# Order of the half-array matmuls in a hybrid decoder layer: neighbours at other tile positions

## The chip, the core and the metric

The kernel runs on one core of one Trainium2 chip. The metric is the device time of one launch in microseconds (us). Three runs of the kernel before gave 1041.28, 1041.54 and 1042.14 us; the median is 1041.54 us.

## What is computed

One decoder layer on 1024 tokens of width 1024, in float32.

```python
h = rms_norm(x, norm_mix_g);  z = h @ w_in                 # 1024 x 1792
q, k, v, u, gate = split(z)                                # 8 query heads, 2 kv heads, 512 + 512 conv channels
a = sliding_window_gqa(rms_norm(q), rms_norm(k), v, sinks, rel_bias)
#   per block of 128 queries: scores against the block before and its own (256 keys),
#   plus bias, softmax with a sink, times v
c = silu(layer_norm(causal_depthwise_conv31(u * sigmoid(gate)) + b))
x = x + concat(rms_norm(a), rms_norm(c)) @ w_out
x = x + square(relu(rms_norm(x) @ w_up)) @ w_down          # hidden width 4096
```

## The kernel before

Everything is kept transposed: channels on the 128 partitions, tokens along the free dimension. Large products split each float32 operand into a high and a low part and use three float32r matmuls of 128x128 by 512 columns (`mm3`, `prod`); these make up nearly all of TensorE's work. Three smaller kinds of matmul are float32 and use a part of the 128x128 array. Each such float32 matmul stands in the trace as two instructions, each with its own weight load.

A matmul that reads operands from partitions 0 to 63 and writes to PSUM partitions 0 to 31 works in the part of the array at row 0, column 0. This pair of row and column is called its *tile position* here, written (row, column); it follows from the partitions that the slices in the code name.

- **Convolution** (`conv`, L423 to L450). The depthwise convolution of 128 channels is done as 64-row matmuls with 32 output partitions. There are four kinds, for r = 0, 1 (upper and lower 64 partitions) and s = 0, 1: position (64 r, 64 r + 32 s). A call makes two halves (`jh`); a half makes 16 matmuls for each of the four kinds, 64 in all, 128 instructions. They write two PSUM tiles, called x (r = 0) and o (r = 1). `conv` is called for four groups of channels, so there are 8 halves and 1024 instructions. Before them DVE transposes into `ha` (L429), and four DMAs (L430) copy parts of it to other partitions.
- **Scores** (`attn_a`, L557 to L580). A unit is one head pair j and one pair of query blocks bp; there are 16 units. A unit makes four matmuls of 64 rows and 128 columns: two blocks for kv group g = 0 at position (0, 0), two for g = 1 at (64, 0). Each group has its own PSUM tile `sc`, of which there are two. ACT and DVE then read each block (L577, L578).
- **Value products** (`attn_c`, L608 to L630). A unit makes up to eight matmuls of 128 rows and 64 columns into PSUM tile `o`: two blocks, two groups g at (0, 64 g), and two key blocks c that accumulate.

What sets the order: the string `SCHED` gives the order in which the dense work, the attention units and the norms are emitted; a list scheduler with its own model of time then places each emitted instruction in its engine's queue, by priority and by when it expects the operands. An engine takes its queue in order. So the order in the code is a wish, and the order that was built is shown below where it matters.

Of the kernel before, what the change touches and what calls it, by code (L numbers as in the profile page):

```python
# [14 lines left out]
AF = mybir.ActivationFunctionType  # L15
# [3 lines left out]
P = 128  # L19
# [48 lines left out]
class Builder:  # L68
# [354 lines left out]
    def conv(self, ct):  # L423
        nc = self.nc
        tw, ha, hg = self.tw[ct], self.ha, self.hg[ct]
        for s in range(2):
            for r in range(2):
                c0, p0 = 64 * r + 32 * s, 64 * r + 32 * (1 - s)
                nc.vector.transpose(ha[c0:c0 + 32, s].rearrange("p b j -> p (b j)"), hg[c0:c0 + 32])  # L429
                self.dma(ha[p0 + 2:p0 + 32, s, 1:NTB + 1, :], ha[c0 + 2:c0 + 32, s, 0:NTB, :])  # L430
        yt = self.tmp("yt", (P, TB, NTB))
        for jh in range(2):
            js = slice(16 * jh, 16 * jh + 16)
            ps = [self.psum("x"), self.psum("o")]
            for s in range(2):
                for j in range(16):
                    for r in range(2):
                        gp, c0 = slice(64 * r, 64 * r + 64), 64 * r + 32 * s
                        nc.tensor.matmul(ps[r][c0:c0 + 32, j * TB:(j + 1) * TB], tw[gp, s, 16 * jh + j, :],
                                         ha[gp, s, 1:NTB + 1, 16 * jh + j], start=True, stop=True)  # L440
            for r in range(2):
                gp = slice(64 * r, 64 * r + 64)
                nc.scalar.copy(yt[gp, js].rearrange("p j b -> p (j b)"), ps[r][gp])
        if ct + 1 < NCT:
            self.conv_load(ct + 1)
        src = yt.rearrange("p j b -> p b j")
        for h in range(2):
            y = self.mp.tile([P, HT], F32, tag="y", name=self.nm("y"), bufs=8)
            self.y[ct, h] = y
            nc.vector.transpose(y.rearrange("p (b t) -> p b t", t=TB), src[:, 16 * h:16 * h + 16, :])  # L450
# [106 lines left out]
    def attn_a(self, j, bp):  # L557
        nc = self.nc
        assert {j, 4} <= self.emitted
        u = dict(j=j, bp=bp, i=sum(self.n_unit))  # L560
        self.n_unit.append(1)
        u["s"] = s = self.tmp("s", (P, 4, 256))
        u["mx"] = mx = self.small("mx", 4)
        for g in range(2):
            gp = slice(64 * g, 64 * g + 64)
            psv = self.psum("sc").rearrange("p (b w) -> p b w", b=2)
            for b2 in range(2):
                b = 2 * bp + b2
                W = P if b == 0 else 2 * P
                k0 = (b + 1) * P - W  # L570
                nc.tensor.matmul(psv[:, b2, 256 - W:], self.Q[b // 4][gp, j, b % 4 * P:(b % 4 + 1) * P], self.kh[gp, k0:k0 + W],
                                 start=True, stop=True)
            for b2 in range(2):
                b = 2 * bp + b2
                W = P if b == 0 else 2 * P
                sl = s[:, 2 * b2 + g, 256 - W:]
                nc.scalar.activation(sl, psv[:, b2, 256 - W:], AF.Copy, scale=self.rq[:, j, b, g:g + 1])  # L577
                nc.vector.tensor_tensor_reduce(sl, sl, self.bias[g][:, j, 256 - W:], 1.0, NEG,  # L578
                                               ALU.add, ALU.max, mx[:, 2 * b2 + g:2 * b2 + g + 1])
        return u  # L580
# [27 lines left out]
    def attn_c(self, u):  # L608
        nc = self.nc
        s, j, bp = u["s"], u["j"], u["bp"]  # L610
        assert 5 in self.emitted
        self.n_attn[bp // 2] += 1
        po = self.psum("o")
        pT = self.tmp("pT", (P, 2, HT))
        for c in range(2):
            ps = self.psum("tr")
            i0 = 2 if bp == 0 and c == 0 else 0
            for i in range(i0, 4):
                nc.tensor.transpose(ps[:, i * P:(i + 1) * P], s[:, i, c * P:(c + 1) * P], self.ident)
            self.evac(EVAC.get(u["i"], "aaa")[c], pT[:, c, i0 * P:], ps[:, i0 * P:])  # L620
        for b2 in range(2):
            b = 2 * bp + b2
            for g in range(2):
                gp = slice(64 * g, 64 * g + 64)
                i = 2 * b2 + g
                c0 = 1 if b == 0 else 0
                for c in range(c0, 2):
                    nc.tensor.matmul(po[gp, b2 * P:(b2 + 1) * P], self.v[:, b - 1 + c, gp], pT[:, c, i * P:(i + 1) * P],
                                     start=c == c0, stop=c == 1)
        self.evac(EVAC.get(u["i"], "aaa")[2], self.Q[bp // 2][:, j, bp % 2 * 256:(bp % 2 + 1) * 256], po[:, :2 * P])  # L630
# [527 lines left out]
```

## Time and profile before

| What | Value |
|---|---|
| median of three runs | 1041.54 us |
| the profiled execution's own time | 1041.51 us |
| its span, first to last instruction | 1039.5 us |
| TensorE (PE) busy | 1009.7 us, 97% of the span |
| VectorE (DVE) busy | 676.9 us, 65% |
| ScalarE (ACT) busy | 489.9 us, 47% |
| mean granted clock of TensorE | 0.979 of full speed |

The 2.0 us between the span and the run's own time lie outside the instructions. TensorE's busy time is the union of its matmuls; matmuls overlap in it, so a busy stretch is not yet one at full pace. The granted clock has two levels, 1.00 and 0.50 in the rows (2.4 and 1.2 GHz); a value between them is a mean over a stretch with both.

### The profile page before, as it was taken

How to read it: one execution, taken by the hardware profiler on the slowest of the kernel's cores; microseconds unless marked ns; L12 is line 12 of the kernel's file. 1: busy time of each engine (PE TensorE's matmuls, PEld its weight loads, DVE VectorE, ACT ScalarE, POOL GpSimd, SP SyncE). 2: the span in 40 equal slices, each digit the busy share in tenths (PEclk: the TensorE clock that was granted, in tenths of full speed). 3: DMA queues.
4: the chain of work that ended last, by engine and by line, in shares of the span. 5: the costliest groups of instructions: out<-in, count | busy, mean ns of one | idle time of the engine just before them, and what ended most of it. 6: DMA issues, size and time to landing. Idle time of an engine off the chain costs nothing.

```text
span 1039.5 us, 14869 instructions
## 1 busy us (share of the span) xinstructions
PE 1009.7 (97%) x5552; PEld 818.4 (79%) x5552; DVE 676.9 (65%) x1148; ACT 489.9 (47%) x944; POOL 117.0 (11%) x87
## 2 busy tenths in 40 slices
PE   6999999989989989999999999999999999999998
PEld 4888887777766777877888888888888888888886
DVE  7456344346766566489778777777784677747763
ACT  5323212777756544466445445445454343443452
POOL 5000012055423530400000000000000000000000
PEclk9999999989987999999999999999999999999999
DMA  9124220000210133436465656576776542336441
GB/s 342 42 61 136 97 72 11 11 21 31 82 61 11 61 112 127 159 133 220 162 235 201 229 207 205 199 244 247 272 274 212 187 144 81 121 107 239 162 162 41
DMA packets 67752, 148.72 MB, mean 143 GB/s; under 512 B 7808, under 2 KB 8576, under 8 KB 67168
## 3 DMA queue, kind: packets, MB, share of 16 engines
q1 hardware_dynamic: 67536, 147.75, 41.5%
q8 instruction: 44, 0.72, 0.3%
q14 instruction: 28, 0.23, 0.1%
q10 hardware_dynamic: 144, 0.02, 0.0%
HBM read 106.98 MB, written 38.80 MB: 140 GB/s over the span
## 4 chain that ended last, share of the span: by engine, by line
PE 87%; DVE 6%; ACT 4%; issue 2%; DMA 1%; SPq 0%; DVEq 0%; POOL 0%; ACTq 0%; POOLq 0%
PE mm L198 7%; PE mm L200 7%; PE mm L199 6%; PE sc L841 4%; PE sc L840 4%; PE sc L842 4%; PE tr L840 3%; PE tr L841 3%; PE tr L842 3%; PE mm L840 3%; PE mm L842 3%; PE mm L841 3%; PE mm L1060 2%; PE mm L1062 2%; PE mm L1061 2%; PE sc L1062 2%
## 5 line engine op out<-in xcount | busy, mean ns | idle before, releaser
L766 ACT CAST wb<-wd 128x512 fp32r<-128x512 f32 x80 | 49.8, 622 | 111.3 <-DVE wd L1028 41.6
L767 DVE TENSOR_TENSOR wb<-wd,wb 128x512 fp32r<-128x512 f32 x80 | 55.3, 691 | 69.9 <-ACT wb L766 69.9
L200 PE MATMUL mm<-xh,wlo 128*128 128x512 f32 x192 | 77.7, 405 | 0.0
L198 PE MATMUL mm<-xh,whi 128*128 128x512 f32 x192 | 77.6, 404 | 0.0
L199 PE MATMUL mm<-xl,whi 128*128 128x512 f32 x192 | 77.2, 402 | 0.0
L767 DVE TENSOR_TENSOR wb<-hb,wb 128x512 fp32r<-128x512 f32 x112 | 76.6, 684 | 0.0
L168 DVE TENSOR_TENSOR wlo<-raw,whi 128x512 fp32r<-128x512 f32 (+1 forms) x54 | 55.0, 1019 | 33.2 <-ACT whi L167 27.9
L167 ACT CAST whi<-raw 128x512 fp32r<-128x512 f32 (+1 forms) x54 | 42.9, 795 | 68.5 <-PE mm L199 46.7
L840 PE MATMUL sc<-op,wb 128*128 128x512 f32 x192 | 74.7, 389 | 0.0
L841 PE MATMUL sc<-op,wb 128*128 128x512 f32 x192 | 74.7, 389 | 0.0
L842 PE MATMUL sc<-op,wb 128*128 128x512 f32 x192 | 74.7, 389 | 0.0
L766 ACT CAST wb<-hb 128x512 fp32r<-128x512 f32 x112 | 69.0, 616 | 0.3 <-PE sc L842 0.3
L766 ACT CAST wb<-raw 128x512 fp32r<-128x512 f32 x46 | 27.7, 621 | 65.2 <-PE tr L842 25.1
L200 PE MATMUL mm<-mix,wlo 128*128 128x512 f32 x128 | 52.1, 408 | 2.0 <-DVE wlo L168 2.0
L198 PE MATMUL mm<-mix,whi 128*128 128x512 f32 x128 | 52.9, 416 | 1.1 <-ACT x1g L766 0.7
L199 PE MATMUL mm<-mix,whi 128*128 128x512 f32 x128 | 52.1, 407 | 0.0
L1061 PE MATMUL mm<-wb,wb 128*128 128x512 f32 x128 | 49.8, 389 | 0.0
L1061 PE MATMUL sc<-wb,wb 128*128 128x512 f32 x128 | 49.8, 389 | 0.0
L840 PE MATMUL tr<-op,wb 128*128 128x512 f32 x128 | 49.8, 389 | 0.0
L841 PE MATMUL tr<-op,wb 128*128 128x512 f32 x128 | 49.8, 389 | 0.0
L1062 PE MATMUL mm<-wb,wb 128*128 128x512 f32 x128 | 49.6, 389 | 0.0
L1062 PE MATMUL sc<-wb,wb 128*128 128x512 f32 x128 | 49.6, 389 | 0.0
(270 smaller groups left out, 2595.1 us busy)
## 6 DMA issues: line engine op xcount, KB each, us to landing
hb<-hid SPq DMA_DIRECT2D x112, 256.0 KB, 2.9
wd<-w_down SPq DMA_DIRECT2D x80, 256.0 KB, 4.0
raw<-w_up SPq DMA_DIRECT2D x27, 512.0 KB, 3.6
hid<-h SPq DMA_DIRECT2D x48, 256.0 KB, 2.9
pa<-pa SPq DMA_DIRECT2D x20, 512.0 KB, 4.9
raw<-w_out SPq DMA_DIRECT2D x32, 256.0 KB, 2.6
hid<-pa SPq DMA_DIRECT2D x32, 256.0 KB, 3.0
hid<-tu SPq DMA_DIRECT2D x32, 256.0 KB, 3.7
```

Of the source, the lines that this page charges most:

```text
L167: nc.scalar.copy(hi, raw)
L168: eng.tensor_tensor(lo, raw, hi.bitcast(F32), ALU.subtract)
L198: nc.tensor.matmul(ps, w[0][:, ws], xh, start=first, stop=False)
L199: nc.tensor.matmul(ps, w[0][:, ws], xl, start=False, stop=False)
L200: nc.tensor.matmul(ps, w[1][:, ws], xh, start=False, stop=last)
L766: self.pin(self.nc.scalar.copy(hi, src))
L767: self.pin(eng.tensor_tensor(lo, src, hi.bitcast(F32), ALU.subtract))
L840: nc.tensor.matmul(ps, wh[:, c], xh, start=first and k == 0, stop=False, skip_group_check=True)
L841: nc.tensor.matmul(ps, wh[:, c], xl, start=False, stop=False, skip_group_check=True)
L842: nc.tensor.matmul(ps, wl[:, c], xh, start=False, stop=last and k == len(xs) - 1, skip_group_check=True)
L1061: nc.tensor.matmul(pss[m], wh[:, c], bl, start=False, stop=False, skip_group_check=True)
L1062: nc.tensor.matmul(pss[m], wl[:, c], bh, start=False, stop=f == NP - 1, skip_group_check=True)
```

## The change

The same matmuls with the same operands and results are issued in another order. In `conv` the loop over s moves inside the loop over j: four neighbours go to (0, 0), (64, 64), (0, 32), (64, 96), where before all 32 matmuls of s = 0 came first, alternating between (0, 0) and (64, 64), and then the 32 of s = 1. In `attn_a` both PSUM tiles are taken first and the groups alternate. In `attn_c` the loop over g moves innermost, so that neighbours go to (0, 0) and (0, 64).

```diff
@@ conv
-            for s in range(2):
-                for j in range(16):
+            for j in range(16):
+                for s in range(2):
                     for r in range(2):
                         gp, c0 = slice(64 * r, 64 * r + 64), 64 * r + 32 * s
                         nc.tensor.matmul(ps[r][c0:c0 + 32, j * TB:(j + 1) * TB], tw[gp, s, 16 * jh + j, :],
...
@@ attn_a
+        psv = [self.psum("sc").rearrange("p (b w) -> p b w", b=2) for _ in range(2)]
+        for b2 in range(2):
+            b = 2 * bp + b2
+            W = P if b == 0 else 2 * P
+            k0 = (b + 1) * P - W
+            for g in range(2):
+                gp = slice(64 * g, 64 * g + 64)
+                nc.tensor.matmul(psv[g][:, b2, 256 - W:], self.Q[b // 4][gp, j, b % 4 * P:(b % 4 + 1) * P], self.kh[gp, k0:k0 + W],
+                                 start=True, stop=True)
         for g in range(2):
-            gp = slice(64 * g, 64 * g + 64)
-            psv = self.psum("sc").rearrange("p (b w) -> p b w", b=2)
-            for b2 in range(2):
...
-                nc.tensor.matmul(psv[:, b2, 256 - W:], self.Q[b // 4][gp, j, b % 4 * P:(b % 4 + 1) * P], self.kh[gp, k0:k0 + W],
-                                 start=True, stop=True)
             for b2 in range(2):
...
@@ attn_c
-            for g in range(2):
-                gp = slice(64 * g, 64 * g + 64)
-                i = 2 * b2 + g
-                c0 = 1 if b == 0 else 0
-                for c in range(c0, 2):
+            c0 = 1 if b == 0 else 0
+            for c in range(c0, 2):
+                for g in range(2):
+                    gp = slice(64 * g, 64 * g + 64)
+                    i = 2 * b2 + g
                     nc.tensor.matmul(po[gp, b2 * P:(b2 + 1) * P], self.v[:, b - 1 + c, gp], pT[:, c, i * P:(i + 1) * P],
                                      start=c == c0, stop=c == 1)
```

The scheduler's own placing moves too. TensorE, the first half of the first convolution, before (x and o are the convolution's PSUM tiles, mm a dense one; L439 is the convolution):

```order
L198 MATMUL mm_794<-xh_253,whi_569 128x512
L439 MATMUL x_355<-ha,tw_121 32x32 x3
L439 MATMUL o_356<-ha,tw_121 32x32 x3
L439 MATMUL x_355<-ha,tw_121 32x32
L439 MATMUL o_356<-ha,tw_121 32x32
```

The same place now:

```order
L198 MATMUL mm_794<-xh_253,whi_569 128x512
L439 MATMUL x_355<-ha,tw_121 32x32
L199 MATMUL mm_794<-xl_254,whi_569 128x512
L200 MATMUL mm_794<-xh_253,wlo_570 128x512
L198 MATMUL mm_794<-xh_271,whi_569 128x512
L439 MATMUL o_356<-ha,tw_121 32x32
L199 MATMUL mm_794<-xl_272,whi_569 128x512
L200 MATMUL mm_794<-xh_271,wlo_570 128x512
L198 MATMUL mm_820<-xh_133,whi_569 128x512
L199 MATMUL mm_820<-xl_134,whi_569 128x512
L200 MATMUL mm_820<-xh_133,wlo_570 128x512
L439 MATMUL x_355<-ha,tw_121 32x32 x4
```

One matmul of x and one of o now stand alone between dense ones, and the other 62 follow together. Counted over the program, the convolution's matmuls stood in 10 uninterrupted runs (64, 64, 64, 64, 64, 64, 47, 17, 5 and 59 long) and stand in 18 now (1, 1, 62, 64, 64, 2, 62, 64, 64, 2, 21, 41, 1, 11, 19, 2, 1 and 30).

TensorE, the first unit's scores (sc, L571), before, where g = 0 (sc_1753) and g = 1 (sc_1760) stand in one run after the convolution:

```order
L505 MATMUL tr_1583<-bones,sq_1524 128x2 x4
L571 MATMUL sc_1753<-kh,Q_497 128x128
L571 MATMUL sc_1753<-kh,Q_497 128x256
L571 MATMUL sc_1760<-kh,Q_497 128x128
L571 MATMUL sc_1760<-kh,Q_497 128x256
L198 MATMUL mm_1555<-xh_253,whi_1344 128x512
```

And now (g = 1 is sc_1754), inside the last half of the convolution:

```order
L439 MATMUL x_1270<-ha,tw_1059 32x32
L571 MATMUL sc_1753<-kh,Q_497 128x128
L439 MATMUL o_1271<-ha,tw_1059 32x32
L439 MATMUL x_1270<-ha,tw_1059 32x32
L571 MATMUL sc_1754<-kh,Q_497 128x128
L571 MATMUL sc_1753<-kh,Q_497 128x256
L439 MATMUL o_1271<-ha,tw_1059 32x32
L571 MATMUL sc_1754<-kh,Q_497 128x256
L439 MATMUL x_1270<-ha,tw_1059 32x32
```

The four scores stood next to each other and are now in three pieces between the convolution's. Of the other 15 units, the second one's scores are cut in two pieces; three (the third, eighth and twelfth) stand in one run before and now; one (the eleventh) stood in one run and is now cut in two by one dense matmul; and the groups of the rest stand apart in both orders. Where the last units' scores were single matmuls between transposes, most now stand in pairs.

## Rows read from the trace of the kernel before

**Rows 1.** The page: span, TensorE's busy time, its granted clock in 40 slices.

```profile
span 1039.5 us, 14869 instructions
PE 1009.7 (97%) x5552; PEld 818.4 (79%) x5552; DVE 676.9 (65%) x1148; ACT 489.9 (47%) x944; POOL 117.0 (11%) x87
...
PEclk9999999989987999999999999999999999999999
```

**Rows 2.** Windows by stage: stretch, length; busy PE, PEld, DVE, ACT, POOL; clock, DMA, GB/s.

```profile
66.00:160.00 94.00, 94.00 (x1314) 80.30 (x1313) 41.17 (x46) 25.48 (x40) 2.90 (x1) 0.98 0.28 90
160.00:230.00 70.00, 63.24 (x331) 52.02 (x330) 28.42 (x85) 39.59 (x86) 17.45 (x17) 0.93 0.05 16
...
305.00:323.00 18.00, 17.75 (x72) 12.45 (x72) 8.04 (x22) 9.50 (x29) 8.05 (x6) 0.53 0.05 15
...
440.00:1040.00 600.00, 592.81 (x2612) 488.89 (x2611) 429.40 (x681) 274.32 (x477) 0.00 (x0) 1.00 0.55 187
```

**Rows 3.** Windows of line 439 alone, the convolution's second half: PE, PEld, clock.

```profile
74.80:79.00 4.20, 3.58 (x128) 3.42 (x128) 1.00 0.01 4
```

**Rows 4.** Timeline of TensorE, the same half: start us, us, instruction.

```profile
74.50 0.39 PE L198 MATMUL mm<-xh,whi 128*128 128x512 f32 x1
74.73 0.39 PE L199 MATMUL mm<-xl,whi 128*128 128x512 f32 x1
75.05 0.22 PE L439 MATMUL x<-ha,tw 64*32 64x32 f32 x1
75.06 0.22 PE L439 MATMUL o<-ha,tw 64*32 64x32 f32 x1
...
76.62 0.23 PE L439 MATMUL x<-ha,tw 64*32 64x32 f32 x1
...
76.64 0.22 PE L439 MATMUL x<-ha,tw 64*32 64x32 f32 x1
...
76.68 0.23 PE L439 MATMUL x<-ha,tw 64*32 64x32 f32 x1
...
76.69 0.23 PE L439 MATMUL x<-ha,tw 64*32 64x32 f32 x1
...
76.74 0.23 PE L439 MATMUL x<-ha,tw 64*32 64x32 f32 x2
...
76.80 0.23 PE L439 MATMUL x<-ha,tw 64*32 64x32 f32 x2
...
78.39 0.23 PE L439 MATMUL x<-ha,tw 64*32 64x32 f32 x1
...
78.56 0.50 PE L200 MATMUL mm<-xh,wlo 128*128 128x512 f32 x1
```

**Rows 5.** Chain that ended last, scores' runs: start us, us, instructions.

```profile
163.42 0.86 PE sc L571 x8
...
234.43 1.06 PE sc L571 x4
...
269.77 1.07 PE sc L571 x8
...
323.59 0.62 PE sc L571 x2
```

**Rows 6.** The same chain, runs of value products.

```profile
253.13 1.02 PE o L628 x12
...
263.32 0.86 PE o L628 x12
...
328.86 0.36 PE o L628 x2
...
330.57 1.02 PE o L628 x14
...
345.84 1.08 PE o L628 x16
```

More of the change, by code (lines that the diff above doesn't have):

```diff
@@ L563, in attn_a @@
         u["mx"] = mx = self.small("mx", 4)
-        for g in range(2):
-            gp = slice(64 * g, 64 * g + 64)
-            psv = self.psum("sc").rearrange("p (b w) -> p b w", b=2)
-            for b2 in range(2):
-                b = 2 * bp + b2
-                W = P if b == 0 else 2 * P
-                k0 = (b + 1) * P - W
-                nc.tensor.matmul(psv[:, b2, 256 - W:], self.Q[b // 4][gp, j, b % 4 * P:(b % 4 + 1) * P], self.kh[gp, k0:k0 + W],
-                                 start=True, stop=True)
+        psv = [self.psum("sc").rearrange("p (b w) -> p b w", b=2) for _ in range(2)]
[7 more added lines that the diff above has]
+                                 start=True, stop=True)
+        for g in range(2):
             for b2 in range(2):
@@ L576, in attn_a @@
                 sl = s[:, 2 * b2 + g, 256 - W:]
-                nc.scalar.activation(sl, psv[:, b2, 256 - W:], AF.Copy, scale=self.rq[:, j, b, g:g + 1])
+                nc.scalar.activation(sl, psv[g][:, b2, 256 - W:], AF.Copy, scale=self.rq[:, j, b, g:g + 1])
                 nc.vector.tensor_tensor_reduce(sl, sl, self.bias[g][:, j, 256 - W:], 1.0, NEG,
```

## Prediction

> **What bounds the kernel now.** I read the page first: TensorE is busy for 1009.7 of 1039.5 us, and its clock is full in nearly every slice [rows 1]. So TensorE's own time is the kernel's time, and what it saves is saved if no other engine is late instead. Then the windows by stage [rows 2]: the convolution lies between 66 and 160 us, where TensorE has no idle time at all (94.00 of 94.00 us) and DVE (41.17) and ACT (25.48) have room. From 160 to 230 us TensorE idles for 6.8 of 70 us; after 440 us it idles for 7.2 of 600. The changed matmuls are in the first two of these stages and in the attention up to 372 us.
>
> Next I looked at one half of the convolution, 128 instructions. Alone, it keeps TensorE busy for 3.58 us [rows 3]. In the timeline [rows 4] the dense matmul ahead starts at 74.73, the first convolution instruction at 75.05, the last at 78.39, the next dense one at 78.56. The run takes 78.56 - 75.05 = 3.51 us. x and o start together, 0.01 us apart (75.05, 75.06): upper and lower rows of the array work side by side. But one position takes its next instruction only after some 0.056 us: from 76.64 to 78.39 are 31 steps, 1.75 / 31 = 0.0565. Two positions at that pace make one instruction per 0.028 us.
>
> The middle of that run is the key view. At 76.64 an x instruction starts only 0.02 us after the one at 76.62, and from there x shows two streams: 76.62, 76.68, 76.74, 76.80 and 76.64, 76.69, 76.74, 76.80 [rows 4]. The first is the end of s = 0 at (0, 0), the second the start of s = 1 at (0, 32). Counting from 75.05, the 29th of the 32 s = 0 instructions starts at 76.62, so three were still to come when s = 1 began. For about 0.17 us four positions (o does the same) work at once, each at its old pace of 0.05 to 0.06 us. The change asks for that state all the time.
>
> **The change part by part.** No instruction is added or removed; DVE, ACT, POOL and DMA do the same work. All costs are starts on TensorE.
>
> *Convolution.* With four positions at 0.0565 us each takes 32 instructions: 31 x 0.0565 + 0.17 (from last start to the next dense one) = 1.92 us instead of 3.51, or 1.59 less. Eight halves: 12.7 us less. Against that stands the order that was built: 18 runs instead of 10. A run costs on entering 75.05 - 74.73 = 0.32 us where a dense step costs 74.73 - 74.50 = 0.23, so 0.09, and on leaving 0.17 - 0.06 = 0.11. Several of the new runs have one or two matmuls and fill one or two positions, so I take 0.25 us for each of the eight: +2.0. Sum -10.7 us. Bounds: the trace has four positions at work only for 0.17 us and not 3.5. If the pace cannot be held, nothing is gained (0, and the 2.0 us of splits lost); more than four times one position cannot be had, and without the splits it is -12.7.
>
> *What waits for the convolution.* In the new order all four kinds start together, so the first needs the copies for s = 1 too, and the next DVE transposes into `ha` are free only at a half's end instead of in its middle. This is 1.9 us after its start, where s = 0 was through at 76.80 - 75.05 = 1.75 before. I cost this at nothing: the new order puts more dense matmuls ahead of two of the halves. Without that cover it costs some tenths per call, below 2 us in all.
>
> *Scores.* Here the change mostly doesn't do what it says. Where both groups stand together, eight instructions took 1.07 us before (0.86 with the short first block), the same as four of one group alone, 1.06 [rows 5]: the groups already overlapped although two of one group came first. For ten of sixteen units the built order keeps the groups apart. What changes is where runs are cut: the eleventh unit becomes two runs (+1.06), the first unit's 0.86 becomes three pieces of at most 0.62 us, the row with two instructions (up to +1.0; I take +0.8, since two of its blocks are short), the second unit's 1.07 becomes 0.62 and 1.06 (+0.6). Among the last units single matmuls become pairs: two runs of 0.62 make one of 1.06 three times (-0.2 each), and about four cuts of the transposes go (-0.1 each, an estimate from the 0.09 and 0.11 above). Net +1.4 us, between 0 and +2.5.
>
> *Value products.* A full unit of 16 instructions takes 1.08 us, and that is 8 per position at 0.11: both positions are busy to the end already. Gains remain where one position ran alone: one unit of 12 took 1.02 against 0.86 in others, and four units that stood as 2 + 14 instructions (0.36 + 1.02) become 4 + 12 (0.37, one pair of starts later by 0.01, + 0.86) [rows 6]. 4 x 0.15 + 0.16 + some 0.05 in each of the others = -1.3 us, between 0 and -2.
>
> Sum: -10.7 + 1.4 - 1.3 = -10.6 us. The profiled execution took 1041.51 us (2.0 of it outside the span), the median is 1041.54, so no correction is needed: 1041.5 - 10.6 = 1030.9, rounded to **1031 us**.
>
> *A rule that speaks against it.* The rows show (0, 0) and (0, 32), which read the same 64 rows, taking instructions side by side at 76.62 to 76.80 us [rows 4]. The Trainium skill, "TensorE: Matmul & The Clock Gate", Part 3, says that a weight load overlaps a running matmul only where their row groups differ. By that rule s = 0 and s = 1 would take turns; the sum would be no gain in the convolution, about 1043 us. The trace, with both streams near 0.055 us per step, does not agree with it over those four steps.
>
> **The rivals.**
>
> *R1, issue is the limit (ends on the other side).* The 0.028 us per instruction may be what the engine can take in, not what two positions can work off. Those four overlapping streams could be a short store of instructions already taken in. For it: the pace of 0.028 is held through all eight halves, and the store is short (three per position). Against it: s = 0 had three waiting in each of two positions, so intake was ahead of the work, not behind it. If it holds at 0.028, the convolution saves nothing, the splits cost 2.0, scores and values nearly cancel: 1041.5 + 2.0 + 1.4 - 1.3 = 1043.6. It decides from about 0.026 us per instruction: there 1024 x 0.002 = 2 us pay just for the splits. Were taking turns among four positions slower than among two, say 0.032 us, it would be 1024 x 0.004 = 4 us more, 1047. The same page of the Trainium skill ("Wait - 56ns, not 53.3ns?") puts the least distance of two starts at about 0.025 us. By that alone an estimate for the convolution is 1024 x 0.025 = 25.6 against 8 x 3.34 = 26.7 us, and the time 1042.3; the 0.01 us between x and o disagrees for single pairs, and no row shows it for a longer stretch.
>
> *R2, half the gain.* Four positions work, but at a pace between, for instance 0.020 us per instruction (128 x 0.020 + 0.17 = 2.73, eight times 0.78 = 6.2 less, 2.0 more): 1037. Or TensorE's gain is lost from 160 to 230 us, where it already idles 6.8 us and ACT is busy for 39.59 of 70 [rows 2]: if half of the 10.6 us is waited off there, 1036. Against it: ACT's work in that stretch hangs on TensorE's results, which come earlier too.
>
> *R3, the clock.* From 305 to 323 us the granted clock is 0.53, nearly all at the lower level, 1.2 GHz, in a stretch of transposes, scores and value products after idle time [rows 2]. The order changes there. One more such stretch takes 18 x 0.47 = 8.5 us: 1039.5. One fewer gives 1022.5. For it: small matmuls and waits stand in the same places; against: most of the order there is unchanged.
>
> **How the numbers follow.** A measurement of this kernel tells 0.2%, about 2.1 us, from no change. My forecast (1027 to 1035) has 0.55, R2 0.17, R1 0.20, R3 0.08. R1 is half within 0.2% and half slower than that; R3's costly side stands at the edge of 0.2%, half to each. So faster 0.55 + 0.17 + 0.04 = 0.76, taken as 0.74, same 0.15, slower 0.11. The range, 1027 to 1043, takes in the forecast's own range, R2, R3's costly side and the nearer half of R1.
>
> **What would show it.** Right: a half of the convolution in one run takes about 1.9 us from first start to next dense start, four positions step at 0.057 us, the ends of the convolution stage move some 10 us earlier, and all later stages keep their length. Wrong at the first step: 3.3 to 3.5 us per half. Wrong at the second: halves of 1.9 us and a stage from 160 to 230 that has grown by what was saved. Wrong by the clock: other slices below full in the clock row of the page. Scores' runs should not be shorter than 1.06 us for four or eight full instructions, value products' 16 not shorter than 1.03.

## The result and the profile after

The changed kernel took 1027.13 us, the median of four executions (1022.59, 1024.94, 1029.32 and 1029.82); the kernel before, beside it, 1041.84. The ratio is 0.9854, 95% interval [0.9818, 0.9889]: 14.7 us less where 10.6 were forecast. The four executions are two pairs. The upper pair ran at a mean granted clock of 0.979, as the kernel before did in its profile; the lower pair at 0.987 and 0.988. The profile after is of the upper pair (1029.32 us), so it shows 12.2 of the 14.7 us and not the rest.

From the page after: the span, TensorE's busy time and its granted clock in 40 slices. They answer to [rows 1].

```profile
span 1027.3 us, 14871 instructions
PE 999.9 (97%) x5552; PEld 807.0 (79%) x5552; DVE 677.0 (66%) x1148; ACT 489.9 (48%) x944; POOL 117.1 (11%) x87
PEclk9999989999969999999999999999999999999999
```

TensorE is busy for 9.8 us less and is still 97% of the span. Its clock row has a 6 in the twelfth slice, which begins at 283 us, where before the twelfth and thirteenth stood at 8 and 7 for the stretch from 305 to 323 us.

Windows by stage of the changed kernel, columns as in [rows 2]:

```profile
66.00:146.00 80.00, 79.83 (x1204) 65.18 (x1204) 38.86 (x44) 24.33 (x38) 2.90 (x1) 1.00 0.33 106
146.00:216.00 70.00, 66.10 (x425) 53.18 (x425) 29.26 (x84) 38.58 (x84) 15.98 (x16) 0.93 0.04 12
290.00:313.00 23.00, 20.18 (x83) 14.84 (x83) 11.86 (x35) 11.31 (x33) 8.33 (x7) 0.55 0.07 24
428.00:1028.00 600.00, 592.67 (x2611) 488.72 (x2610) 429.53 (x681) 274.38 (x477) 0.00 (x0) 1.00 0.55 186
```

The last stage is unchanged (592.67 busy of 600). The stage behind the convolution idles 3.9 of 70 us, against 6.8 before. The two windows hold 425 and 331 matmuls, so they don't compare the same work; over the whole span TensorE's busy time falls by 9.8 and the span by 12.2, so 2.4 us of idle time went. What was saved in the convolution was not waited off behind it. The third row is the stretch at half clock, to which I come back.

One half of the convolution, TensorE's timeline after (start us, us, instruction), and line 439's window around it; compare [rows 4] and [rows 3]:

```profile
75.91 0.39 PE L198 MATMUL mm<-xh,whi 128*128 128x512 f32 x1
76.23 0.22 PE L439 MATMUL x<-ha,tw 64*32 64x32 f32 x1
76.24 0.22 PE L439 MATMUL o<-ha,tw 64*32 64x32 f32 x1
76.24 0.22 PE L439 MATMUL x<-ha,tw 64*32 64x32 f32 x1
76.25 0.22 PE L439 MATMUL o<-ha,tw 64*32 64x32 f32 x1
76.28 0.24 PE L439 MATMUL x<-ha,tw 64*32 64x32 f32 x1
...
78.14 0.31 PE L439 MATMUL x<-ha,tw 64*32 64x32 f32 x3
78.38 0.50 PE L199 MATMUL mm<-xl,whi 128*128 128x512 f32 x1
```

```profile
76.00:78.60 2.60, 2.22 (x128) 2.04 (x128) 1.00 0.03 6
```

Four instructions start within 0.02 us and the next four follow 0.05 us later: four positions work side by side for the whole run. It takes 78.38 - 76.23 = 2.15 us instead of 3.51. That is more than the 1.92 forecast: the step of one position is (2.15 - 0.17) / 31 = 0.064 us and not 0.0565.

The half that waited, same columns:

```profile
88.49 0.39 PE L198 MATMUL mm<-xh,whi 128*128 128x512 f32 x1
88.97 0.27 PE L439 MATMUL x<-ha,tw 64*32 64x32 f32 x2
89.17 0.27 PE L439 MATMUL o<-ha,tw 64*32 64x32 f32 x2
89.50 0.28 PE L439 MATMUL x<-ha,tw 64*32 64x32 f32 x4
89.81 0.23 PE L439 MATMUL o<-ha,tw 64*32 64x32 f32 x2
```

Its first eight instructions need 89.81 - 88.97 = 0.84 us: each kind waits for its own copy into `ha`, and these land one after the other (at 88.72, 89.03, 89.36 and 89.67 us). The run takes 2.84 us, 0.69 more than its neighbours.

The chain of waits after, scores (L571) and value products (L629), against [rows 5, 6]:

```profile
147.85 0.63 PE sc L571 x3
148.70 1.15 PE sc L571 x2
...
183.68 0.63 PE sc L571 x2
...
217.30 1.06 PE sc L571 x4
...
230.35 0.81 PE o L629 x12
...
258.61 1.07 PE sc L571 x8
...
334.39 1.02 PE o L629 x16
```

Eight score instructions of two groups take 1.07 us and four of one group 1.06, as before. Sixteen value products take 1.02 us (1.08 before) and twelve 0.81 (0.86 to 1.02).

To see where the 12.2 us of the profiled pair went, I gave the time from each start on TensorE to the next start to the instruction that began it, and summed by line (worked out from all instructions of the two traces):

| Kind of instruction | before | after | difference |
|---|---|---|---|
| convolution | 28.57 | 19.38 | -9.2 |
| scores | 30.56 | 32.53 | +2.0 |
| value products | 21.19 | 19.39 | -1.8 |
| transposes L619, L694, L676; sums L505, L645 | 48.27 | 42.66 | -5.6 |
| dense products in three passes, attention side (`mm3`) | 272.40 | 274.66 | +2.3 |
| the two late stages (308 and 310 us) | 617.89 | 617.96 | +0.1 |

The unchanged small kinds lose mostly waits, and some time at half clock. The whole time at half clock is about the same, 44.6 and 42.6 us.

The stretch at half clock and what stands ahead of it, TensorE in the changed kernel:

```profile
289.37 0.66 PE L620 MATMUL tr<-ident,s 128*128 128x128 f32 x4
292.59 1.94 PE L620 MATMUL tr<-ident,s 128*128 128x128 f32 x8 [2.57 <-DVE pT L607]
...
300.19 2.07 PE L571 MATMUL sc<-kh,Q 64*128 64x256 f32 x4
```

And in the kernel before:

```profile
299.81 0.66 PE L619 MATMUL tr<-ident,s 128*128 128x128 f32 x4
303.69 1.06 PE L619 MATMUL tr<-ident,s 128*128 128x128 f32 x8 [3.23 <-DVE pT L606]
...
310.49 2.07 PE L571 MATMUL sc<-kh,Q 64*128 64x256 f32 x4
```

In both TensorE idles, in brackets, for a copy of `pT` on DVE. The clock falls to its lower level (1.2 GHz) at 291.8 us in the changed kernel, 0.75 us before this idle time ends, and at 305.4 us in the kernel before, 1.7 us after it has ended; it stays there for 20.5 and 17.1 us. Four score instructions then take 2.07 instead of 1.06 us. DVE in the changed kernel shows why the copy is late, with the POOL instruction beside it:

```profile
288.34 1.93 POOL L603 TENSOR_TENSOR s<-s,rd 128x1024 f32<-128x1024 f32 x1 [4.30 <-DVE rd L598]
288.45 2.10 DVE L579 CUSTOM_DVE_ANT_0 s<-s,bias 128x256 f32<-128x256 f32 x1
...
291.77 0.68 DVE L607 COPY pT<-tr 128x512 f32<-128x512 f32 x1
```

DVE works in order. The copy stands behind four score biases and an addition, and one of the biases takes 2.10 us where its neighbours take about 0.42. It starts 0.11 us after the POOL instruction and ends 0.28 us after that one's end. This is a pattern: in the changed kernel 16 of the 64 biases take over 0.7 us, in the kernel before 15, and each of them ends 0.28 to 0.29 us after the end of a POOL instruction that it ran beside. Twelve short biases also overlap a POOL instruction, so overlap alone is not enough. That POOL is what holds DVE up is read from the traces alone; no run moved POOL's work. The idle time is 0.66 us shorter after than before.

### The profile page after: what moved, and what is told of

It reads as the page before. It is cut to its first block, busy times and chain, and to the rows that moved or that the text cites. A ratio compares the mean times of both kernels' runs of the same rounds, so it can differ in the third digit from the quotient of the medians.

```text
span 1027.3 us, 14871 instructions
## 1 busy us (share of the span) xinstructions
PE 999.9 (97%) x5552; PEld 807.0 (79%) x5552; DVE 677.0 (66%) x1148; ACT 489.9 (48%) x944; POOL 117.1 (11%) x87
## 4 chain that ended last, share of the span: by engine, by line
PE 86%; DVE 7%; ACT 4%; issue 2%; DMA 1%; SPq 1%; DVEq 0%; POOL 0%; ACTq 0%
PE mm L198 7%; PE mm L200 6%; PE mm L199 6%; PE sc L843 4%; PE sc L842 4%; PE sc L841 4%; PE tr L843 3%; PE tr L842 3%; PE tr L841 3%; PE mm L841 3%; PE mm L843 3%; PE mm L842 3%; PE mm L1061 3%; PE mm L1063 3%; PE mm L1062 3%; PE sc L1062 2%
## 5 line engine op out<-in xcount | busy, mean ns | idle before, releaser
L168 DVE TENSOR_TENSOR wlo<-raw,whi 128x512 fp32r<-128x512 f32 (+1 forms) x54 | 55.1, 1021 | 25.8 <-ACT whi L167 20.5
L579 DVE CUSTOM_DVE_ANT_0 s<-s,bias 128x256 f32<-128x256 f32 (+1 forms) x64 | 42.6, 697 | 11.0 <-ACT s L578 10.7
L1062 PE MATMUL mm<-wb,wb 128*128 128x512 f32 x128 | 49.8, 389 | 0.0
```

Source lines behind the costliest of these rows:

```text
L168: eng.tensor_tensor(lo, raw, hi.bitcast(F32), ALU.subtract)
L1062: nc.tensor.matmul(pss[m], wh[:, c], bl, start=False, stop=False, skip_group_check=True)
```

## Experiments

Theory A for the convolution: four positions work side by side, each at its own pace. Its rivals were issue (R1) and turns of neighbours on the same rows. Theory A for the rest: the clock's long stretch comes from the idle time ahead of it. Its rival: it comes with the kind of instructions there. A ratio is to the kernel before on the same chip.

**The convolution's loops alone** (of the change's diff only the part in `conv`).

> The convolution's loop alone as changed, scores and value products as before. Theory A (the convolution's starts give the deterministic part, and what went beyond it is the clock): 9.2 us less on line 439 as in the changed kernel's trace, so about 1032 us in executions with a mean granted clock near 0.979, and about 5 us less in any execution near 0.987. Rival B (what went beyond the convolution came from the reordered value products and the placing of the transposes): 1032 us in every execution, clock 0.979, with no spread over 2 us.

Measured: 1031.4 us (four executions, 1030.42 to 1031.82, clock 0.980 to 0.982), ratio 0.9905 [0.9891, 0.9919]. The convolution takes 19.48 us on TensorE, 9.1 less, and the time falls by 9.9. All four stand in one group, so this is what the expectation's rival had; the executions near a clock of 0.987 that theory A allowed did not come. The scores' line costs 33.48 us here, 2.9 more than before, although the scores' code is that of before.

**The value products' loops alone** (only the part in `attn_c`).

> The value products' loop alone as changed. Theory A: 1.8 us less on their line as in the changed kernel's trace, so about 1039.7 us at clock 0.979. Rival B: 1036 to 1038 us, since then this part carries the 3 us that the transposes and norms lost as well.

Measured: 1034.25 us, ratio 0.9953 [0.9933, 0.9972], in two groups: 1039.4 to 1039.7 at clock 0.980 (three executions) and 1033.1 to 1034.4 at 0.987 to 0.990 (five). The value products themselves give 21.19 - 18.89 = 2.3 us, with 1.0 us less of it at half clock. The window, same columns and stretch as the third row of [rows 2], and TensorE behind its idle time, from an execution of the lower group:

```profile
305.00:323.00 18.00, 17.30 (x98) 12.13 (x99) 12.69 (x30) 11.04 (x33) 10.45 (x7) 0.91 0.06 15
```

```profile
303.82 1.07 PE L619 MATMUL tr<-ident,s 128*128 128x128 f32 x8 [2.54 <-DVE pT L606]
...
309.82 1.13 PE L571 MATMUL sc<-kh,Q 64*128 64x256 f32 x4
```

The clock is 0.91 where it was 0.53: it falls for 3.4 us and comes back, and the scores run at full clock. The idle time ahead is 2.54 us, 0.69 shorter than before. So a lower group like that of the changed kernel comes with the value products; with the convolution alone none of four executions was in one.

**The scores alone** (only the part in `attn_a`).

> The scores' loop alone as changed. Theory A: 2.0 us more on their line by the changed kernel's trace, of which some came from being cut by the convolution; without that 1 us more, about 1042.5 us at clock 0.979. Rival B: the same or less than before, 1040 to 1041.5, because single scores between transposes were joined.

Measured: 1040.97 us (1038.42 to 1042.74), ratio 0.9993 [0.9983, 1.0002]: no change. Line 571 takes 30.33 us, 0.2 less. The +2.0 us of the changed kernel on that line are not the scores' own edit.

**Convolution and value products, scores of before.**

> Convolution and value products as changed, scores as before. Theory A: 9.2 + 1.8 = 11 us less, about 1030.5 us at clock 0.979, some 2 us better than the whole change at the same clock; in executions near 0.987 about 1025. Rival B: equal to the whole change, 1027 to 1029, in every execution.

Measured: 1027.24 us, ratio 0.9865 [0.9839, 0.9891], again in two groups, 1030.1 to 1030.5 (clock 0.978, 0.979) and 1022.95 to 1024.4 (0.987 to 0.990), three executions each. The two parts together are the whole change.

**The late copy on ACT**, once in the changed kernel and once in the kernel before:

```diff
-EVAC = {... 8: 'vaa', ...}
+EVAC = {... 8: 'aaa', ...}
```

> The changed kernel, but the ninth attention unit's first copy out of PSUM (L607, EVAC entry 8) is done by ACT and not by DVE. In the changed kernel TensorE idles 2.57 us for that copy at 290 us, and the granted clock falls to its lower level there for 20.5 us. Theory A (the fall follows the idle time, and how long it lasts makes the spread): without the idle time the clock stays full there, mean 0.987 or more in every execution, and 1021 to 1024 us without the two groups near 1023 and 1029. Rival C (the fall comes from the small matmuls that stand there): still two groups, near 1023 and 1029 us.

> The kernel before with the same copy moved from DVE to ACT. There the idle time was 3.23 us at 300 us, and the lower level lasted 17.1 us. Theory A: 1035 to 1037 us, mean clock 0.987. Rival C: 1040 to 1042 us, clock 0.98.

Measured: before with this edit 1035.56 us, ratio 0.9948 [0.9929, 0.9967], five of six executions at clock 0.986 or 0.987; the long stretch is 6.8 instead of 17.1 us. TensorE there:

```profile
300.57 0.63 PE L619 MATMUL tr<-ident,s 128*128 128x128 f32 x4 [0.93 <-POOL s L602]
301.89 0.65 PE L619 MATMUL tr<-ident,s 128*128 128x128 f32 x4 [0.69 <-ACT pT L606]
303.67 1.87 PE L645 MATMUL o<-ones,nacc 128*128 128x1 f32 x8 [1.12 <-DVE nacc L641]
```

All 5552 matmuls of this kernel stand in the order of the kernel before; what differs is that the idle time of 3.23 us is broken into pieces with matmuls between them. So here the rival by the kind of instructions is out. The changed kernel with the edit took 1027.75, ratio 0.9868 [0.9849, 0.9888], all at 0.982 or 0.985: no gain. In its profile the stretch is 10.2 us, and three others of 6.8 stand elsewhere. There the edit also changed TensorE's order, so it decided nothing for that kernel.

**The convolution's order at the same positions**, with the value products of the change and the scores of before. First r outside s, so that neighbours share rows in pairs, (0, 0), (0, 32), (64, 64), (64, 96):

```diff
-                for s in range(2):
-                    for r in range(2):
+                for r in range(2):
+                    for s in range(2):
```

> Convolution and value products as changed, scores as before, but the convolution's neighbours go to (0, 0), (0, 32), (64, 64), (64, 96): pairs on the same rows follow each other. Theory A (four positions run at 16 ns per instruction whatever the order among them): a half of 128 instructions in 2.15 us, 1023 to 1030 us as with the other order. Rival D (a weight load has to wait for a running matmul on the same rows): slower, between 2.15 and 3.5 us per half, 1028 to 1038.

Measured: 1029.4 us, ratio 0.989 [0.9872, 0.9908], all five at clock 0.978 to 0.980. The same half as in the profile after, line 439's window:

```profile
75.40:77.80 2.40, 2.00 (x128) 1.84 (x128) 1.00 0.02 7
```

From its first start to the next dense one it takes 1.93 us. That is the predicted 1.92 to 0.01 us, by the order that the rule on row groups should have slowed; neither expectation had it faster than 2.15. Second, the same loops as in the change but both backwards:

```diff
-                for s in range(2):
-                    for r in range(2):
+                for s in (1, 0):
+                    for r in (1, 0):
```

> Convolution and value products as changed, scores as before, but s and r count downwards in the convolution, so that the first matmul of a half needs the copy that lands last; the built order has 16 runs instead of 19 and six of eight halves whole or nearly so. Theory A (short runs cost 0.2 us each, and one half lost 0.7 us to copies that had not landed): line 439 in 18.5 to 19 us instead of 19.6, the time lower by 0.5 to 1 us at the same clock. Rival E (the dense matmuls moved ahead of the convolution only move the wait): the same within 0.5 us.

Measured: 1028.02 us (1024.29 to 1032.45), ratio 0.9872 [0.9845, 0.9899]; a half takes 1.97 us, the one that waits 3.00. Line 439 took 18.96 us, as expected, but the time did not fall below that of convolution and value products (1027.24). Here rows alternate as in the change, so sharing rows is not what makes 2.15 into 1.93. Why the change's own order is the slowest of the three stays open. Its pace is not fixed either: the run of 124 at 69.03 us in the profile after takes 1.98 us, a step of (1.98 - 0.17) / 30 = 0.060 us.

**Two positions on the same rows only** (r outermost, then j, then s, in the kernel before):

```diff
-            for s in range(2):
-                for j in range(16):
-                    for r in range(2):
+            for r in range(2):
+                for j in range(16):
+                    for s in range(2):
```

> Only the convolution's loops differ from the kernel before: r outermost, then j, then s, so that neighbours lie at two positions that read the same rows, (0, 0) and (0, 32), and later (64, 64) and (64, 96). Theory A (a position takes one instruction per 0.056 us, whichever rows it reads, and positions work side by side): two positions give 0.028 us per instruction, a half takes 3.5 us as before, and the time is that of the kernel before, within 0.2%. Rival (same-row neighbours take turns, as the rule on row groups has it): 0.056 us per instruction or slower, a half takes 7 us, eight halves 28 us more, about 1069 us. Rival (rows shared by two positions are read once and faster): below 3 us per half, a shorter stage than before.

Measured: 1042.54 us, ratio 1.0012 [1.0001, 1.0024], within 0.2%. A half in one run, line 439's window:

```profile
98.00:102.00 4.00, 3.58 (x128) 3.41 (x128) 1.00 0.28 75
```

It is the 3.58 us of [rows 3] to the digit, with 3.505 us from first start to next dense start. Two positions take 0.027 us per instruction here, as on different rows (3.51 / 128). Other halves took up to 3.74 us, 0.029 each, with no single step above 0.07 us; why is open. The 7 us of taking turns came nowhere.

**Filling the idle time with useless work.** The transposes that stand ahead of the idle time are repeated 16 times, same operands and same place in PSUM, once in the kernel before, once in the changed one and once in the kernel with r outside s:

```diff
                 nc.tensor.transpose(ps[:, i * P:(i + 1) * P], s[:, i, c * P:(c + 1) * P], self.ident)
+            for k in range(16 if u["i"] == 8 and c == 1 else 0):
+                i = k % 4
+                nc.tensor.transpose(ps[:, i * P:(i + 1) * P], s[:, i, c * P:(c + 1) * P], self.ident)
```

> The kernel before, with the ninth unit's second set of four transposes followed by 16 repeats of the same transposes (same operands, same place in PSUM), some 2.3 us of useless work that stands where TensorE idled for 3.2 us before the long stretch at half clock near 305 us. Theory A (idle time ahead is what lets the clock fall there): the idle is filled, the stretch of 17.1 us becomes 7 us or less, the mean clock is 0.986 or more, and the time is 1033 to 1037, although work was added. Rival B (the clock falls by the kind of instructions there, not by the idle time): the stretch stays at 17 us, and the time is 1041 to 1044.

> The changed kernel with the same 16 repeated transposes, where it idles for 2.6 us before its stretch of 20.5 us at half clock near 292 us. Theory A (idle time): no execution, or few, with the long stretch; clocks of 0.986 or more, 1019 to 1024 us, one group instead of two. Rival B: the two groups stay, 1023 to 1025 and 1029 to 1031, or move up by the up to 2.3 us that were added.

> The convolution in the order r, s (half of its neighbours on the same rows, 1.93 us per half), the value products of the change, the scores of before, and the same 16 repeated transposes. Without them this kernel took 1029.4 us with every execution at a clock of 0.980 or less. Theory A (idle time): clock 0.986 or more, 1018 to 1023 us, the fastest of all. Rival B: 1029 to 1032.

Measured in the changed kernel: 1025.11 us, ratio 0.984 [0.9821, 0.9859]; all five executions lie between 1023.6 and 1025.31. TensorE there (the line numbers are three higher), and the window that answers to the third one of the profile after:

```profile
289.87 0.66 PE L620 MATMUL tr<-ident,s 128*128 128x128 f32 x4
290.36 1.91 PE L623 MATMUL tr<-ident,s 128*128 128x128 f32 x16
293.08 0.63 PE L620 MATMUL tr<-ident,s 128*128 128x128 f32 x4 [0.81 <-DVE pT L607]
...
300.38 1.13 PE L571 MATMUL sc<-kh,Q 64*128 64x256 f32 x4
```

```profile
290.00:313.00 23.00, 20.50 (x128) 14.53 (x129) 15.91 (x41) 13.01 (x39) 10.25 (x8) 0.93 0.08 24
```

Nothing was removed and 16 matmuls were added. The order built near them is not quite the same: four score instructions now stand behind the transposes that they stood ahead of, and ACT does one copy of `pT` later. The idle time is 0.81 instead of 2.57 us, the clock over these 23 us 0.93 instead of 0.55, and no execution is above 1025.4 where half of the changed kernel's are above 1029. The rival, under which the two groups stay, is out as far as five executions show it. Of the 4.1 us between the two profiles' spans, 3.0 are on the scores' line and 0.8 in the convolution, whose copies into `ha` were in time in this execution (2.09 us for that half).

In the kernel before: 1037.96 us (1034.96 to 1039.78), ratio 0.9961 [0.9948, 0.9973]. Its idle time went only from 3.23 to 1.49 us; the long stretch became one of 6.8 and one of 3.4 us, and the clocks spread from 0.982 to 0.988. It is faster, by less than the 1033 to 1037 us expected. TensorE there:

```profile
301.82 1.91 PE L622 MATMUL tr<-ident,s 128*128 128x128 f32 x16
305.23 0.63 PE L619 MATMUL tr<-ident,s 128*128 128x128 f32 x4 [1.49 <-DVE pT L606]
```

With r outside s: 1026.53 us (1025.05 to 1027.27), ratio 0.9858 [0.9838, 0.9877], 2.9 less than without the repeats but not the fastest. Its stretch is 10.2 us in spite of 0.82 us of idle time, and the mean clock 0.983 to 0.985. The expected 1018 to 1023 was missed. So the idle time is not the whole condition.

Taken together (idle time ahead of the stretch, and the executions at a clock of 0.985 or more, which stands in for a short stretch, since each kernel has one profile; the two kernels with the copy on ACT are left out, since their idle time stands in pieces of up to 1.12 us):

| Kernel | idle, us | executions at 0.985 or more |
|---|---|---|
| before (the 53 beside the experiments) | 3.23 | 2 of 53 |
| convolution alone; scores alone; two positions on the same rows | 3.22, 3.23, 3.23 | 0 of 4; 0 of 11; 0 of 11 |
| value products alone | 2.54 | 5 of 8 |
| convolution and value products | 2.54 | 3 of 6 |
| the change | 2.57 | 2 of 4 |
| the change's convolution backwards | 2.57 | 3 of 6 |
| r outside s | 2.56 | 0 of 5 |
| before, filled | 1.49 | 6 of 12 |
| the change, filled | 0.81 | 4 of 5 |
| r outside s, filled | 0.82 | 2 of 4 |

The profiles show something else that goes with the length: when the clock falls. In the five with 20.5 us (the change, its convolution backwards, r outside s, convolution and value products, two positions on the same rows) the clock fell 0.2 to 1.2 us before the idle time ended; in the three with 17.1 us (before, convolution alone, scores alone) it fell 1.5 to 1.7 us after its end. In the value products alone, with 2.54 us of idle time, it fell 2.1 us after the end, and the stretch was 3.4 us. What sets the moment of the fall no run shows.

Of the kernels tried, the changed one with repeated transposes has the lowest median and beats the kernel before by 1.6%. Its interval overlaps that of the change alone; what the five executions show is none above 1029 us.

## Why the prediction was off, step by step

**The failed step is R3, the clock.** I gave it 0.08, wrote that "most of the order there is unchanged", and put it at nothing in the sum. Its faster side ("one fewer") came in two of the four executions, at a clock of 0.987 and 0.988. Neither was profiled; that they lack the long stretch is read from the clock and from the profile of the value products alone, which is of their lower group and has 3.4 us. What was wrong was the condition. I looked for a change of order inside the stretch, where in fact little changed, and not at the idle time of 3.23 us ahead of it, one row above in the trace. The value products made that idle time 0.66 us shorter, and about half of the executions then run at the higher clock (with r outside s none of five). The value products alone show it (1033.1 to 1034.4 or 1039.4 to 1039.7), breaking the idle time into pieces in the kernel before cuts the stretch to 6.8 us at the same order on TensorE, and with the idle time of the changed kernel filled none of five executions is in the slower group. The median of 1027.13 is the mean of an execution of either pair. Of the 4.1 us by which the forecast was off, 2.5 come from this (14.7 - 12.2) and 1.6 from the terms below. The price of 8.5 us was too high as well: the two pairs differ by 5.8 us, the groups of the value products alone by 5.9, those of convolution and value products by 6.9. That the "1022.5" for one stretch fewer was nearly met (1022.59 and 1024.94) is luck: this price was too high and the rest of the sum too small.

**Convolution: forecast -10.7, measured -9.2; mechanism right, size off.** Four positions do work side by side, but in this order the step per position is 0.064 us and not 0.0565: three of the four halves that stand in one run of 128 take 2.15 us. By that eight halves give 8 x 1.36 = -10.9 us, the late copies take 0.7 back, and +1.0 is left, where I had taken +2.0 for the splits. This is a remainder and was not measured by itself; 1.2 us of the convolution also ran at half clock. Where r lies outside s the 1.92 us are met (1.93). One sample of four overlapping steps [rows 4] gave the right pace for the array and not for every order. This error and the clock have opposite signs.

**The copies into `ha`: forecast at nothing, measured +0.7 us**, in the one half that starts at 88.97 us. The cover by dense matmuls held for the others. The bound of 2 us held.

**Scores: forecast +1.4, measured +2.0** on their line, in the bounds. The reading that the groups overlapped before was right: alone, the edit does nothing (0.9993). By unit, the first costs 1.3 us more in its three pieces (0.8 forecast, part of it at half clock), the second 0.6 and the eleventh 1.05 as forecast; the last units and the sixth give 1.0 back. None of this needs the scores' edit: with the scores of before, convolution and value products show the same three.

**Value products: forecast -1.3, measured -1.8**, in the bounds, at the same clock. Twelve take 0.81 us, and sixteen 1.02, where I had said not below 1.03.

**What the sum did not have:** the other small kinds lose 5.6 us and the dense products of that part cost 2.3 more. Most of the 5.6 comes with the convolution's loops: with these alone the same kinds lose 5.0 us. I had costed waits behind the convolution as a possible loss (R2); they became shorter, by 2.4 us over the span. With it the profiled pair comes to -12.2 at the same clock, against -10.6.

**R1, issue,** is out: 128 instructions in 1.93 us are 0.015 us each. The Trainium skill's "TensorE: Matmul & The Clock Gate", section "Wait - 56ns, not 53.3ns?", puts the least distance of two starts at about 0.025 us; with four tile positions the trace does not agree. (By its own terms the prediction's time for that rule is 1043.6 - 1.1 = 1042.5, not 1042.3, and its 1047 is 1047.6.) The rule of Part 3 of that page of the Trainium skill, that a weight load overlaps only a matmul of another row group, isn't borne out either: two positions on the same rows took 3.505 us for 128 instructions, in which weight loads were busy for 3.41 us, and two on different rows 3.51. **R2** is out as well: no half at a pace between, and nothing was lost behind the convolution.

Open remain: why the change's order of four positions steps at 0.064 us and two others at 0.057 to 0.058; what sets the moment at which the clock falls, and with it how long it stays low in executions of one kernel; and why the kernel with r outside s, with the same 2.56 us of idle time, never ran above a clock of 0.980.

## What to carry to other kernels

Small matmuls that fill a part of the array gain when neighbours in the queue lie at different tile positions, and only up to the number of positions that were not yet at work: here two became four in the convolution, and for scores that already overlapped nothing came. Try the orders of the positions on the chip, since they differ by a tenth. And ahead of a stretch at half clock look for the idle time of TensorE, and for what the engine that it waits for is itself held up by. Filling the idle time with useless matmuls took 3.9 us off the kernel before, and less, 2.0 us with overlapping intervals, off the changed one.

## What was not expected of the hardware

Adding 16 useless transposes (1.91 us on TensorE) made the kernel before faster (ratio 0.9961 [0.9948, 0.9973]); in the changed kernel the granted clock over 23 us went from 0.55 to 0.93. With the same idle time of about 2.55 us ahead, the stretch at the lower level was 20.5 us long in four profiles and 3.4 in one. And a bias operation on DVE that takes 0.42 us by itself took up to 2.11 beside a POOL instruction, in the kernel before and after; in each of the 14 profiles every such operation of over 0.6 us ends 0.28 to 0.29 us after a POOL instruction.
